# A two-layer decoder trunk: factors through the logarithm of k, transposes by transfers, guarded single buffers, and a new table of distances

## The chip, the cores and the metric

The kernel runs on one core of a Trainium2 chip. A core has a matrix engine (TensorE, "PE" in the profile, with its weight loads as "PEld"), three engines for elementwise work (VectorE "DVE", ScalarE "ACT", GpSimd "POOL"), and SyncE ("SP"), which here only issues transfers. Each engine works through a queue of its own in order, and they wait for one another by semaphores. Transfers are issued from SP's and ScalarE's queues ("SPq", "ACTq"). The metric is the device time of one execution in microseconds; lower is better.

## What is computed

Two layers over 256 tokens of width 2048, in float32. Each layer normalises the residual h, makes one wide input projection, feeds two groups of heads from it, and projects their outputs back:

```python
hn = rms_norm(h, norm_w[l])
proj = hn @ w_in[l]
y_a = deltanet_branch(...)          # 8 heads of 128, gated delta rule
y_b = hgrn2_branch(...)             # 8 heads of 128, gated linear recurrence
h = h + concatenate([y_a, y_b]) @ w_out[l]
gate = sigmoid(h @ w_ple_gate[l])
h = h + (p[l] @ w_ple_up[l]) * gate
...
return rms_norm(h, final_norm_w)
```

In the delta-rule branch ("DN") q and k are divided by their norms, so the sum of squares of each row of q is needed. In the HGRN2 branch ("HG") k = (1 - lb) sigmoid(-f), log f = log(lb + (1 - lb) sigmoid(f)), G is the running sum of log f, and the products inside a chunk are

```python
A = einsum("bhrd,bhsd,bhrsd->bhrs", q_c, k_c, exp(G_r - G_s))   # r >= s
```

## The kernel before

**Products.** The big projections are done in three products each: a weight tile is split into a high part `whi` (ScalarE, line 443) and a rest `wlo` (VectorE, line 445), the activations likewise, and TensorE sums high by high, high by low and low by high (line 381 is the helper that issues every product; line 384 is the helper that issues every transpose). The work is cut into *steps* of one weight tile: `run_step` issues the products of one step, mostly twelve of 128x512. `ahead` loads weight tiles through SP's queue four steps ahead (line 424) and splits them two steps ahead.

**Everything else is woven between the steps.** The mixers are Python generators that emit instructions and then yield a number of steps to wait, or a condition. `tick`, called after each step, counts them down and resumes those that are due. The numbers come from the tables `DELAY` (by kind of generator and place) and `DELAY_AT` (the same for one group, so `"h2u64"` is the place u64 of HG group 2). TensorE's instructions keep exactly the order in which they are emitted; the other engines' queues are ordered by the compiler's scheduler, by readiness and then by order of emission. Where the next step needs a tile that is not emitted yet, `while not pairs_ready(...): tick()` lets turns go by without a step.

**Transposes.** Activations must stand with channels on partitions. This is done in two ways: on TensorE against the identity (`turn`, `turned`, `stat`, and the end of `head_norm`), or by transfers. For the latter, `apart` (line 568) copies the float32 tile into two planes of 16-bit halves on ScalarE and writes them to memory from ScalarE's queue (line 569), and `across` (line 576) reads them back with a transposing transfer on SP's queue. The tuples `FQ_DMA`, `VC_DMA`, `PV_DMA` and `Y_DMA` name the groups that go by transfers. For the residual (`after_out`, which makes `g0` and `g1` for the gate, and `after_gate`, which makes `n1` for the next layer) the quarters c = 0, 1, 2 go by transfers and c = 3 on TensorE.

**DN.** Four groups of two heads in each layer. `decay` makes the table `Dt` (one buffer, tag "Dt"): two products by GpSimd, `pD` on TensorE, an exponential. `dkdq` applies the convolution and SiLU; `k_side` transposes k on TensorE (`ssk`) and scales it by `Dt`; `q_side` makes the Gram products `pg`, the matrix `Bt` and `QK` with `Dt`, then transposes q on TensorE (`ssq`), squares the rows on ScalarE (line 922) and makes `nq`, which scales the output. It then calls `inv.given`; when all four groups have given, `Inverse` runs: small products `pp16` to `px64` with copies between them (lines 776 to 850). After it each group runs its recurrence `pz0`, `pS`, `pw`, `pz1`, `po` and its norm.

**HG.** `f_side` makes k (tag "hk", one buffer) and G ("hG", one buffer); `q_side` makes, for each distance u = 2, 4, ..., 128, a tile of factors `X` (tag "hX", four buffers): two subtractions (lines 1159, 1161; for u = 128 a subtraction and a copy, line 1163), an exponential (line 1164), a multiplication of the lower half by k (line 1166) and of the upper half by q (line 1172). The products go to three banks, `pa` (u = 1 to 8), `pb` (16 to 64) and `pa128`.

Of the kernel before, what the change touches and what calls it, by code (L numbers as in the profile page):

```python
# [17 lines left out]
NG = 4  # L18
# [15 lines left out]
def chunk_cols(chunk):  # L34
# [5 lines left out]
DELAY = {  # L40
# [6 lines left out]
DELAY_AT = {  # L47
# [14 lines left out]
}  # L62


FQ_DMA = 0, 1, 2
VC_DMA = 0, 1
# [112 lines left out]
def trunk(ctx: ExitStack, tc: tile.TileContext, head, xT, x, pT, W, par, fw, cst, msk, eye, out):  # L179
# [137 lines left out]
    lnhd = cp.tile([128, 1], F32, name="lnhd")  # L317
    G.memset(lnhd, float(-0.5 * np.log(128.0)))
    mhalf = cp.tile([128, 1], F32, name="mhalf")
    G.memset(mhalf, -0.5)  # L320
# [96 lines left out]
    LOOK, LOAD = 2, 4  # L417
    state = dict(small=0, next=0, loaded=0, prepped=0, squared=0)

# [433 lines left out]
    class DN:  # L853
# [17 lines left out]
        def decay(self):  # L871

            g, n = self.g, self.n
            self.beta = self.row.beta[:, 4 * g:4 * g + 4]
            ugs = []
            for j in range(2):
# [38 lines left out]
        def stat(self, w, name, tiles=range(4)):  # L915

            ps = pm.tile([128, 512], F32, tag="m", name=self.n + name)
            for i in tiles:
                PE.transpose(ps[:, 128 * i:128 * i + 128], self.kq[i % 2][:, i // 2, w, :], ident)
            ss = small(name)  # L920
            for i in tiles:
                S.activation(sp.tile([128, 128], F32, tag="junk", name="junk", bufs=1), ps[:, 128 * i:128 * i + 128],
                             AF.Square, accum_out=ss[:, i:i + 1])
            return ps, ss

# [29 lines left out]
        def q_side(self):  # L955
            n, kq = self.n, self.kq
            yield self.wait("q")
# [24 lines left out]
            for hh, pg in enumerate(pgs):  # L982
                for t in range(2):
                    i = 2 * hh + t
                    V.scalar_tensor_tensor(Bt[:, i], pg[:, 256 * t:256 * t + 128], nb[:, i:i + 1], Dt[:, i],
                                           ALU.mult, ALU.mult)
                V.tensor_tensor(self.QK[:, 2 * hh:2 * hh + 2], pg.rearrange("p (t w c) -> p t w c", t=2, w=2)[:, :, 1, :],
                                Dt[:, 2 * hh:2 * hh + 2], ALU.mult)
            G.affine_select(self.QK, self.QK, pattern=[[0, 4], [1, 128]], compare_op=ALU.is_ge, fill=0.0, base=0,
                            channel_multiplier=-1)  # L990
            yield self.wait("ssq")
            pq, ss = self.stat(1, "ssq")
            lq = small("lq")
# [85 lines left out]
    class HG:  # L1079
# [9 lines left out]
        def wait(self, step):  # L1089
            return delay("h", self.g, step)  # L1090

        def hi(self, ps, c0):
            self.v = mix("iv", 512, 2, self.n + "iv")
            for t in range(2):
                S.activation(self.v[:, 256 * t:256 * t + 256], ps[t][:, c0:c0 + 256], AF.Copy, scale=self.row.rt[:, t:t + 1])
            self.done.add("i")
            yield 1

        def hfhq(self, ps, c0):
            et, _ = evict(ps, c0, 512, self.row.rt, self.n + "fq")  # L1100
            if self.g in FQ_DMA:
                x = yield from apart(et, self.n + "fq")
                yield self.wait("e")
                t = across(x, self.n + "fq")
                yield self.wait("c")
                spawn(self.f_side(t[:, 0:512]))
                spawn(self.q_side(t[:, 512:1024]))
            else:
                yield self.wait("p")
                spawn(self.f_side(turned(et, 0, self.n + "pf")))  # L1110
                spawn(self.q_side(turned(et, 256, self.n + "pq")))

        def f_side(self, fs):
# [10 lines left out]
            for m in range(2):  # L1124
                sl = slice(256 * m, 256 * m + 256)
                V.tensor_tensor_scan(self.G[:, sl], keep, sg[:, sl], 0.0, ALU.mult, ALU.add)
            self.done.add("f")
            yield self.wait("f")

        def q_side(self, qr):  # L1130
# [8 lines left out]
            yield self.after("f")  # L1139
            k, Gc = self.k, self.G  # L1140
            k4 = v4(k)
# [10 lines left out]
            def factors(us):  # L1152


                X = mix("hX", 512, 4, n + f"X{us[0]}")
                xs = [X[:, 512 * j:512 * j + 512] for j in range(len(us))]
                for u, x in zip(us, xs):
                    ends = lo(Gc, u)[:, :, u - 1:u].to_broadcast([128, 256 // u, u])
                    V.tensor_tensor(lo(x, u), ends, lo(Gc, u), ALU.subtract)
                    if u < 128:  # L1160
# [4 lines left out]
                for u, x in zip(us, xs):  # L1165
                    V.tensor_tensor(lo(x, u), lo(x, u), lo(k, u), ALU.mult)
                    hx = hi(x, u)
# [82 lines left out]
            for b in range(0, 128, 32):  # L1250
                S.copy(A[b:b + 32, :, b:b + 32], Ad[b:b + 32])
            xs = factors((128,))
            yield self.wait("u64")

# [63 lines left out]
    def after_out(c, ps, hact, l):  # L1318
        for m in range(2):
            V.tensor_tensor(h[c][:, m], ps[m], h[c][:, m], ALU.add)  # L1320
        if c < 3:
            hact[2 * c:2 * c + 2] = yield from turn_by_dma(c, f"g{l}", lambda kp: None)
# [4 lines left out]
    def after_gate(c, ps, up, act, st, l):  # L1327
# [21 lines left out]
        if l + 1 < DEPTH:  # L1349
            scales = lambda kp: norm_scales(l + 1, kp)  # L1350
            if c < 3:
                act[2 * c:2 * c + 2] = yield from turn_by_dma(c, f"n{l + 1}", scales)
# [227 lines left out]
```

## Time and profile before

| what | value |
|---|---|
| runs | 1213.8, 1214.54, 1216.82 us; median 1214.54 |
| the profiled execution | 1215.15 us, of which the span from the first to the last instruction is 1213.2 |
| granted TensorE clock, mean | 0.997 |
| moved by transfers | 252.24 MB, mean 208 GB/s |
| transfers of SP's and ScalarE's queues | 61.4% and 5.4% of 16 transfer engines' span |
| VectorE's and ScalarE's largest groups | the weight splits, 481.2 and 408.6 us |

Times in the profile are microseconds, "ns" where marked. Rows of groups read: line, engine, operation, output<-inputs, shapes, count, then busy time, mean of one, and idle time ahead of it with what ended it. Rows of waits read: who <- whom: total, times, longest. Rows of the timeline and of the chain begin with the start and the length. Rows of a tile give the shortest, middle and longest duration in ns, then first and last start. A name such as `hg12X` is HG, layer 1, group 2, tile X. Lengths of products are modelled by the profiler and overlap; distances between starts, and the chain, tell what a product holds TensorE for.

### The profile page before, as it was taken

To read this page: it belongs to the slowest core of one execution; us is meant where nothing else is said; L and a number is where in the kernel's file an instruction comes from. 1 tells how busy PE (TensorE), PEld (TensorE's weight loads), DVE (VectorE), ACT (ScalarE), POOL (GpSimd) and SP (SyncE) were. 2 spreads that over 40 slices of the span, in tenths; PEclk is the share of its full clock that TensorE was granted. 3 is DMA by queue.
4 is the path that set the end of the run, shared out by engine and by line. 5 is a ranking of instruction groups with operands and counts; after the bars stand their busy time and mean duration, and the time that the engine had idled before them with its cause. 6 is when DMAs were issued, how large, how long until landed. Compare 5 with 4: busy or idle time off the path is not lost. (4 is left out here: it accounts for less than half of the span.)

```text
span 1213.2 us, 21302 instructions
## 1 busy us (share of the span) xinstructions
PE 1198.1 (99%) x8098; PEld 997.9 (82%) x8098; DVE 877.1 (72%) x1537; ACT 825.3 (68%) x1424; POOL 78.1 (6%) x67
## 2 busy tenths in 40 slices
PE   9999999999899999999999999999999999999997
PEld 8888888888788888888788888888788888888886
DVE  8669796878768756546665888877897786665565
ACT  7578777678678755538656778766886776564553
POOL 1410000000000000000003100100000000000011
PEclk9999999999999999999999999999999999999999
DMA  8677756686655648756867777667756566596563
GB/s 313 200 244 226 239 191 212 210 239 175 204 174 174 192 157 257 237 191 191 260 213 221 228 231 232 190 192 222 213 171 188 155 193 209 173 279 212 180 205 122
DMA packets 150646, 252.24 MB, mean 208 GB/s; under 512 B 83472, under 2 KB 90000, under 8 KB 150544
## 3 DMA queue, kind: packets, MB, share of 16 engines
q1 hardware_dynamic: 130528, 228.71, 61.4%
q10 hardware_dynamic: 20016, 22.17, 5.4%
q8 instruction: 63, 1.03, 0.3%
q14 instruction: 39, 0.32, 0.1%
HBM read 212.84 MB, written 21.23 MB: 193 GB/s over the span
## 5 line engine op out<-in xcount | busy, mean ns | idle before, releaser
L445 DVE TENSOR_TENSOR wlo<-raw,whi 128x1024 fp32r<-128x1024 f32 (+2 forms) x393 | 481.2, 1229 | 255.8 <-ACT whi L443 247.6
L443 ACT ACTIVATE whi<-raw 128x1024 fp32r<-128x1024 f32 (+2 forms) x393 | 408.6, 1044 | 235.8 <-PE out L381 64.3
L381 PE MATMUL in1hf<-whi,n1hi 128*128 128x512 f32 x128 | 41.0, 402 | 0.8 <-ACT dn12zs L673 0.8
L381 PE MATMUL in1hi<-whi,n1hi 128*128 128x512 f32 x128 | 41.4, 404 | 0.0
L381 PE MATMUL gate<-whi,g0hi 128*128 128x512 f32 x128 | 39.7, 392 | 1.1 <-ACT pg L1334 1.1
L381 PE MATMUL in1dk<-whi,n1hi 128*128 128x512 f32 x128 | 39.9, 393 | 0.0
L381 PE MATMUL in1hi<-whi,n1lo 128*128 128x512 f32 x128 | 39.7, 391 | 0.0
L381 PE MATMUL in1hf<-whi,n1lo 128*128 128x512 f32 x128 | 39.6, 390 | 0.0
L381 PE MATMUL in1dk<-whi,n1lo 128*128 128x512 f32 x128 | 39.5, 390 | 0.0
L381 PE MATMUL gate<-whi,g0lo 128*128 128x512 f32 x128 | 39.4, 389 | 0.0
L381 PE MATMUL in1dv<-whi,n1hi 128*128 128x512 f32 (+1 forms) x128 | 36.6, 378 | 0.0
L381 PE MATMUL in1hf<-wlo,n1hi 128*128 128x512 f32 x128 | 35.7, 390 | 0.2 <-DVE wlo L445 0.2
L381 PE MATMUL gate<-whi,g1hi 128*128 128x512 f32 (+1 forms) x120 | 35.7, 379 | 0.0
L381 PE MATMUL gate<-wlo,g0hi 128*128 128x512 f32 x128 | 35.6, 390 | 0.1
L381 PE MATMUL gate<-whi,g1lo 128*128 128x512 f32 (+1 forms) x120 | 35.7, 379 | 0.0
L381 PE MATMUL in1hi<-wlo,n1hi 128*128 128x512 f32 x128 | 35.6, 390 | 0.0
L381 PE MATMUL in1dk<-wlo,n1hi 128*128 128x512 f32 x128 | 35.6, 389 | 0.0
L381 PE MATMUL in1dv<-whi,n1lo 128*128 128x512 f32 (+1 forms) x128 | 35.0, 365 | 0.0
L381 PE MATMUL gate<-wlo,g1hi 128*128 128x512 f32 (+1 forms) x120 | 32.4, 378 | 0.0
L381 PE MATMUL in1dv<-wlo,n1hi 128*128 128x512 f32 (+1 forms) x128 | 31.5, 363 | 0.0
L381 PE MATMUL in0hi<-whi,n0hi 128*128 128x512 f32 x96 | 30.9, 403 | 0.0
L381 PE MATMUL in0hf<-whi,n0hi 128*128 128x512 f32 x96 | 30.5, 399 | 0.0
(1404 smaller groups left out, 2890.0 us busy)
## 6 DMA issues: line engine op xcount, KB each, us to landing
raw<-W SPq DMA_DIRECT2D x383, 512.0 KB, 3.9
raw<-W SPq DMA_DIRECT2D x7, 544.0 KB, 5.3
h<-x SPq DMA_DIRECT2D x4, 512.0 KB, 4.9
xt<-xT SPq DMA_DIRECT2D x3, 512.0 KB, 5.6
out_dram<-h SPq DMA_DIRECT2D x5, 256.0 KB, 2.3
di0d<-di0Bt ACTq DMA_DIRECT2D x4, 256.0 KB, 2.3
di1d<-di1Bt ACTq DMA_DIRECT2D x4, 256.0 KB, 2.7
fw<-fw ACTq DMA_DIRECT2D x2, 512.0 KB, 3.9
```

Of the source, the lines that this page charges most:

```text
L381: return tc.keep_in_program_order(nc.tensor.matmul(*a, **k))
L443: S.activation(hi[:, sl], raw[:, sl], AF.Copy)
L445: V.tensor_tensor(lo[:, sl], raw[:, sl], hi[:, sl].bitcast(F32), ALU.subtract)
```

## The change

It has five parts.

1. HGRN2's factors hold k through its logarithm: `f_side` adds ln(k + 2^-120) and subtracts it from G into a new tile `Gk`; the lower halves then use `Gk` in place of G, and the multiplication by k at line 1166 goes. `hX` has three buffers in place of four.
2. q's row sums: in all four DN groups (`SSQ_DMA`) q's planes are copied apart by two strided copies, written, transposed by a transfer and squared from there, in place of `stat(1, "ssq")`.
3. The residual's last quarter: `G_DMA` and `N_DMA` name all four quarters, so `turn` is no longer used.
4. Single buffers guarded: `decay` waits until the group before has emitted its last use of `Dt` (`state["dn"]`), and HG's `f_side` and `q_side` start only when the group before has emitted its last factors (`state["hg"]`).
5. The tables of distances are filled anew.

```diff
-    "b2e": 6, "b2g": 6, "b2o": 2,
-    "b3g": 5, "b3o": 2, "b3t": 6,
...
+    "b0e": 9, "b0g": 5, "b0o": 2, "b0t": 5,
+    "b1e": 7, "b1g": 6, "b1o": 5, "b1t": 6,
+    "b2e": 15, "b2g": 6, "b2o": 2, "b2t": 5,
+    "b3e": 8, "b3g": 5, "b3o": 6, "b3t": 8,
...
+SSQ_DMA = 0, 1, 2, 3
+G_DMA = 0, 1, 2, 3
+N_DMA = 0, 1, 2, 3
...
             self.beta = self.row.beta[:, 4 * g:4 * g + 4]
+            yield lambda: state["dn"] == NG * self.l + g
...
+            state["dn"] += 1
             G.affine_select(self.QK, self.QK, pattern=[[0, 4], [1, 128]], compare_op=ALU.is_ge, fill=0.0, base=0,
                             channel_multiplier=-1)
-            yield self.wait("ssq")
-            pq, ss = self.stat(1, "ssq")
+            if g in SSQ_DMA:
+                rows = dr.tile([256 * 512], U16, tag="tr512", name=n + "qd", bufs=4)
+                flat = u16(tmp(n + "qpl"))
+                for t in range(2):
+                    S.copy(flat.rearrange("p (w h t c) -> p w h t c", w=2, h=2, t=2)[:, :, :, t],
+                           u16(kq[t]).rearrange("p h v (c w) -> p w h v c", w=2)[:, :, :, 1])
+                nc.scalar.dma_start(out=rows.rearrange("(p x) -> p x", p=128), in_=flat)
+                yield self.wait("qe")
+                pq = across((rows, 512, 512), n + "q")
+                yield self.wait("qt")
+                ss = self.sums(pq, "ssq", range(4))
...
+                yield self.turn_is_ours
                 spawn(self.f_side(t[:, 0:512]))
...
+            S.activation(sg, self.k, AF.Ln, bias=tiny)
+            self.Gk = mix("hGk", 512, 1, n + "Gk")
+            V.tensor_tensor(self.Gk, self.G, sg, ALU.subtract)
...
-                X = mix("hX", 512, 4, n + f"X{us[0]}")
+                X = mix("hX", 512, 3, n + f"X{us[0]}")
...
-                    V.tensor_tensor(lo(x, u), ends, lo(Gc, u), ALU.subtract)
+                    V.tensor_tensor(lo(x, u), ends, lo(Gk, u), ALU.subtract)
...
-                    V.tensor_tensor(lo(x, u), lo(x, u), lo(k, u), ALU.mult)
...
             xs = factors((128,))
+            state["hg"] += 1
...
-        if c < 3:
+        if c in G_DMA:
             hact[2 * c:2 * c + 2] = yield from turn_by_dma(c, f"g{l}", lambda kp: None)
...
-            if c < 3:
+            if c in N_DMA:
                 act[2 * c:2 * c + 2] = yield from turn_by_dma(c, f"n{l + 1}", scales)
```

More of the change, by code (lines that the diff above doesn't have):

```diff
@@ L318, in trunk @@
     G.memset(lnhd, float(-0.5 * np.log(128.0)))
+    tiny = cp.tile([128, 1], F32, name="tiny")
+    G.memset(tiny, float(2.0 ** -120))
     mhalf = cp.tile([128, 1], F32, name="mhalf")
@@ L417, in trunk @@
     LOOK, LOAD = 2, 4
-    state = dict(small=0, next=0, loaded=0, prepped=0, squared=0)
+    state = dict(small=0, hg=0, dn=0, next=0, loaded=0, prepped=0, squared=0)
     def load(n):
@@ L919, in stat, with sums @@
                 PE.transpose(ps[:, 128 * i:128 * i + 128], self.kq[i % 2][:, i // 2, w, :], ident)
+            return ps, self.sums(ps, name, tiles)
+        def sums(self, ps, name, tiles):
             ss = small(name)
@@ L923, in stat @@
                              AF.Square, accum_out=ss[:, i:i + 1])
-            return ps, ss
+            return ss
         def dkdq(self, ps, c0):
@@ L955, in q_side @@
         def q_side(self):
-            n, kq = self.n, self.kq
+            n, kq, g = self.n, self.kq, self.g
             yield self.wait("q")
@@ L988, in q_side @@
                                 Dt[:, 2 * hh:2 * hh + 2], ALU.mult)
+            state["dn"] += 1
             G.affine_select(self.QK, self.QK, pattern=[[0, 4], [1, 128]], compare_op=ALU.is_ge, fill=0.0, base=0,
                             channel_multiplier=-1)
-            yield self.wait("ssq")
-            pq, ss = self.stat(1, "ssq")
+            if g in SSQ_DMA:
[9 more added lines that the diff above has]
+                ss = self.sums(pq, "ssq", range(4))
+            else:
+                yield self.wait("ssq")
+                pq, ss = self.stat(1, "ssq")
             lq = small("lq")
@@ L1090, in wait, with turn_is_ours @@
             return delay("h", self.g, step)
+        def turn_is_ours(self):
+            return state["hg"] == NG * self.l + self.g
         def hi(self, ps, c0):
@@ L1109, in hfhq @@
                 yield self.wait("p")
+                yield self.turn_is_ours
                 spawn(self.f_side(turned(et, 0, self.n + "pf")))
@@ L1139, in q_side @@
             yield self.after("f")
-            k, Gc = self.k, self.G
+            k, Gc, Gk = self.k, self.G, self.Gk
             k4 = v4(k)
```

24 rows, old and new, of tables (DELAY, DELAY_AT) are left out of this document.

## The prediction

> **What bounds the kernel now.** I read the page first (engine totals, then the slices), then TensorE's waits, then pieces of the chain of work that ended last.
>
> ```profile
> span 1213.2 us, 21302 instructions
> ```
>
> Of this span the engines were busy:
>
> ```profile
> PE 1198.1 (99%) x8098; PEld 997.9 (82%) x8098; DVE 877.1 (72%) x1537; ACT 825.3 (68%) x1424; POOL 78.1 (6%) x67
> ```
>
> TensorE is busy 99% of the span; no other engine passes 72%. A busy share alone proves little, so the next view asks what TensorE ever waited for. These are all its waits of the whole execution:
>
> ```profile
> PE di0px L381 <- ACT di0P L840: 3.1, 2, 2.8
> PE gate L381 <- ACT pg L1334: 1.1, 1, 1.1
> PE warm L381 <- DVE zeros L256: 1.1, 1, 1.1
> PE in1hf L381 <- ACT dn12zs L673: 0.8, 1, 0.8
> PE hg03yp L384 <- DVE hg03yt L655: 0.3, 1, 0.3
> PE hg13yp L384 <- DVE hg13yt L655: 0.3, 1, 0.3
> PE in1hf L381 <- DVE wlo L445: 0.2, 1, 0.2
> PE in0dz L381 <- ACT n0ahi L281: 0.2, 1, 0.2
> ```
>
> They sum to 7.1 us. So the time is the sum of what stands in TensorE's queue, in the order the program writes out. Work taken off that queue is worth its full length; work taken off VectorE, ScalarE or the transfers is worth nothing unless one of these waits shrinks. The price of a piece comes from the chain, where lengths are TensorE time and not an instruction's own duration:
>
> ```profile
> 957.48 0.44 PE dn12pv L384 x4
> 957.92 2.77 PE in1dv L381 x12
> ...
> 1048.62 57.15 PE out L381 x252
> ...
> 1111.21 0.88 PE g1t L384 x8
> ```
>
> L384 is a transpose. Four take 0.44 us, eight take 0.88. Twelve weight products, one step of the loop, take 57.15 / 21 = 2.72 us undisturbed and 2.77 behind an insertion.
>
> **The change, part by part.** *q's row sums.* Eight groups (four pairs of heads, two layers) lose the transposes of `stat(1, "ssq")`:
>
> ```profile
> L384 PE MATMUL dn00ssq<-cs,dn00kq x4: 271/272/273, 109.0 to 109.3; 128*128 128x128 f32 x4
> ```
>
> Four starts within 0.3 us (0.1 apart), and the chain's 0.44 / 4 is 0.11 us each. 8 x 0.44 = 3.5 us leave TensorE. *The residual's last quarter.* `turn` for c = 3 goes in three places (g0, n1, g1) of eight transposes: 3 x 0.88 = 2.65 us. Together 56 transposes, 6.2 us; 11 fewer insertions at 0 to 0.05 us (2.77 against 2.72), taken as 0.03, add 0.3. No part adds a TensorE instruction. Sum so far: **-6.5 us**.
>
> The Trainium skill, page "TensorE: Matmul & The Clock Gate", Part 4, gives about 275 ns for a transpose inside a kernel. The durations above agree (272 ns), and by that price 56 would be worth 15.4 us; but starts 0.11 us apart show that they overlap, so the trace speaks against counting them so.
>
> *What replaces them.* Every transposed tile now goes through ScalarE copies into 16-bit planes, a write to memory, and a transposing transfer on SP's queue. The kernel already does this for three quarters:
>
> ```profile
> L568 ACT COPY n12pl<-h x2: 1030/1036/1042, 592.8 to 593.8; 128x1024 uint16<-128x1024 uint16 x2
> n11d<-n11pl ACTq DMA_DIRECT2D x2, 256.0 KB, 6.6
> g11tr<-g11d SPq DMA_TRANSPOSE x1, 8.2
> ```
>
> Residual: 6 copies x 1.04 = 6.2 us of ScalarE. Row sums: 16 strided copies of 512 values, not in the trace; between half the row above and all of it, 8 to 17 us. With the new logarithm of k below, ScalarE gets 20 to 28 us over the span, and the transfers carry some 7 MB more (8 x 0.25 and 3 x 0.5, written and read). What must hide it is slack beside TensorE, worst where the k/q chunks run:
>
> ```profile
> 60.00:160.00 100.00, 100.00 (x449) 82.81 (x449) 80.62 (x148) 78.94 (x139) 6.34 (x4) 1.00 0.75 237
> ```
>
> (columns: TensorE, weight loads, VectorE, ScalarE, GpSimd, clock, transfer share, GB/s.) ScalarE at 79% rises to about 86%, transfers at 0.75 by some 0.03. I take 0.
>
> Does the data come in time? A step being 2.72 us, I counted the steps between each hand-over in the code. q's row sums feed only `nq`, needed dozens of steps later at the DN output; but `given` now follows them, so the inverse starts three steps later (after step 66 of the run, was 63) and is ready after 105, was 100. The chain of the last DN group does not move: its first product stays after step 129, held by its own v, and its output transpose comes after step 138, was 139. So the later inverse is absorbed. The tightest transposed tile is the residual's last quarter ahead of layer 1:
>
> ```profile
> 614.58 0.69 DVE L1345 TENSOR_TENSOR h<-h,pg 128x512 f32<-128x512 f32 x1
> 602.76 1.71 ACT L533 ACTIVATE n1hi<-n12tr,pr 128x256 fp32r<-128x256 f32 x4 [2.02 <-DMA n12tr<-n12d]
> 634.88 0.66 PE L381 MATMUL in1dz<-whi,n1hi 128*128 128x272 f32 x4
> ```
>
> h is ready at 615.3; a copy behind other work (1 + 1.04), a write (6.6), a transpose (8.2, the longest of the residual's) and the split (1.71 on ScalarE and an estimated half us of VectorE behind it, from 0.69 for twice the columns) end at 634.3 at the worst; the product needs it at 634.0, as 0.88 us go. Cost 0 to 0.3 us; 0 taken. In the gate the same tile has 12 steps, 33 us: free.
>
> *HGRN2.* `lo(k)` no longer multiplies each factor:
>
> ```profile
> L1166 DVE TENSOR_TENSOR hg01X<-hg01X,hg01k x7: 417/420/422, 223.6 to 265.0; 128x256 f32<-128x256 f32 x7
> 314.23 0.63 ACT L1164 ACTIVATE hg02X<-hg02X 128x512 f32<-128x512 f32 x1 [3.08 <-DVE hg02X L1161]
> 314.88 1.18 ACT L840 COPY di0P<-di0pp 64x512 f32<-64x512 f32 x2
> ```
>
> VectorE loses 56 x 0.42 = 23.5 us and gains eight subtractions of 512 columns, at the price of the addition at 614.58 above, 8 x 0.69 = 5.5; ScalarE gains eight logarithms, at the price of the exponential of the same size, 8 x 0.63 = 5.0. All of it lies beside TensorE: worth 0, except that a VectorE chain ahead of a product gets shorter. But `hX` goes from four buffers to three. X16, X32 and X64 fill them, so X128 can start only when the bank `pb` has been multiplied. Before it ran ahead:
>
> ```profile
> 924.80 0.53 PE L381 MATMUL hg12pa<-hg12X 128*32 128x64 f32 x29
> 928.56 0.61 PE L381 MATMUL hg12pa<-hg12X 128*128 128x128 f32 x4
> L1172 DVE TENSOR_TENSOR hg12X<-hg12X,hg12q x7: 416/418/421, 889.8 to 921.7; 128x256 f32<-128x256 f32 x7
> ```
>
> X128's last multiplication started at 921.7, before `pb` ended at 925.3. Now subtraction, copy, exponential and multiplication (0.42 + 0.42 at most + 0.63 + 0.42 = 1.9 us bare, 5.0 with the longest hold above, 3.08) have to fit in the 3.2 us to 928.56. Only the third group has one step there; the others have two. Twice 0 to 1.8 us: 0 to 3.6; I take 0.8, nearer to the bare chain, since the program hands it to the queues ahead of its due time.
>
> *The guards* are waits of the program that emits the instructions, not of an engine; nothing queues behind them. A decay is now written only after the group before has used `Dt`, so D's product moves from after step 21 to after 44 and lands in one gap with the transposes of k and the Gram products: four of the five banks. Bounds 0 to 2 us (a bank freed one copy later); 0 taken, for the next request comes four steps later.
>
> *Distances anew.* Three effects on TensorE's order. The HG output in group 3 gets two steps to its transpose where one was: the two 0.3 us waits go, **-0.5**. The inverse's last hand-over to DN group 0 shrinks from two steps to one:
>
> ```profile
> 316.12 1.09 PE L381 MATMUL di0px<-di0Tt,di0P 64*32 64x64 f32 x62 [0.31 <-ACT di0P L840]
> 319.75 1.17 ACT L850 COPY di0Tt<-di0px 64x512 f32<-64x512 f32 x2
> 911.76 1.10 PE L381 MATMUL di1px<-di1Tt,di1P 64*32 64x64 f32 x64
> 916.54 1.18 ACT L850 COPY di1Tt<-di1px 64x512 f32<-64x512 f32 x2
> ```
>
> The copies end 3.7 and 4.9 us behind the product; with one step and a transpose (3.2 us) in between, TensorE would wait 0.5 and 1.7: 0 to 2.2, as ScalarE's order falls. I take 1.2. The 2.8 us wait for `di0P` has the same one step as before; in layer 1 that cost nothing. Gone or kept, -2.8 to 0; I take -1.4. Some distances overshoot what is left (c = 2 of the residual needs 23 turns where 16 steps remain, its `e` being 15), so `while not pairs_ready` makes 31 turns without products; by my count only splits, output transposes and one DN pair fall into them, none on a tight chain.
>
> Sum: -6.5 - 0.5 - 1.4 + 0.8 + 1.2 = **-6.4 us**. The profiled execution took 1215.15, so 1208.75; the median of the runs shown is 0.61 lower, 1214.54, so **1208.1 us**.
>
> **The rivals.** (1) *The gain is mostly given back*: the new tight places cost their upper bounds (3.6 + 2.2) and the old waits stay, -6.5 + 5.8 = -0.7, so 1213.8 from the median; for it, 31 idle turns and ScalarE at 86%; against, 7 us of waits in all of before. (2) *Weights late behind transposing transfers.* SP's queue issues both, and a transposing issue can stand in it:
>
> ```profile
> 467.97 2.73 SPq L576 DMA_TRANSPOSE g00tr<-g00d  x1
> 470.80 1.00 SPq L424 DMA_DIRECT2D raw<-W  x2
> 471.90 4.49 SPq L576 DMA_TRANSPOSE g01tr<-g01d  x1
> SPq L576 <- DMA n11d<-n11pl: 7.1, 1, 7.1
> 480.57 1.06 ACT L443 ACTIVATE whi<-raw 128x1024 fp32r<-128x1024 f32 x1 [0.46 <-DMA raw<-W]
> 1060.00:1110.00 50.00, 50.00 (x222) 41.39 (x222) 29.47 (x30) 25.84 (x28) 0.00 (x0) 1.00 0.86 258
> ```
>
> After two such issues from 468.0 to 476.4 a weight split was 0.46 us late and TensorE, two splits ahead (5.4 us), did not notice: a stop starts at about 8.4 - 0.46 + 5.4, or 13.4 us. g02 with g03 and n12 with n13 are now written back to back; a wait of 7.1 and two issues of 4.5 make 16.1, so 2.7 us in three places: 1208.1 + 8.1 = 1216.2. Against it stands the last row, a transfer share of 0.86 with TensorE busy all 50 us. The Trainium skill, "DMA: Bandwidth & Descriptors", section "Issuing engines are not separate DMA queues", says that all transfers share the same 16 engines whoever issues them, which speaks for this rival; no row here shows weights losing to a transpose by more than the 0.46 us.
>
> (3) *Slower: ScalarE's queue held by X128.* Its exponential waits for VectorE, which waits for `pb`; behind it stand the copies of `di0P` and `di0Tt`. Before, the hold of 3.08 us at 314.23 above, with the copy of `di0P` right behind it at 314.88, cost TensorE 2.8 us once. By the new order `pb` of group 2, the inverse's last two products, `pa128` and DN 0's first product lie within three steps. Held at all three hand-overs in both layers, 6 x 2.8 = 16.8, less the 3.1 there already: -6.5 + 13.7 = +7.2, so 1221.7 from the median. It decides from 3.2 us a layer. (4) *Each transpose is worth its duration*, 56 x 0.272 = 15.2, so 1199.3; the chain speaks against it.
>
> **How the numbers follow.** Forecast 1208.1 (1203 to 1211): 0.70. Rival 1: 0.16. Rival 2: 0.05. Rival 3: 0.07. Rival 4: 0.02. The range 1203 to 1216 takes in the forecast with all old waits gone (-6.5 - 4.5, so 1203.5) and rivals 1 and 2; about 0.1 and some tails lie outside. About 0.3% (3.6 us) is what a measurement of this kernel can tell from no change: faster (under 1210.9) 0.71, same 0.21, slower (over 1218.2) 0.08.
>
> **What would show it.** Transposes at L384's place: 88 where 144 stood, no `ssq`, `g0t`, `g1t`, `n1t` among TensorE's rows; TensorE's busy time down by 6 to 7 us and its list of waits between 4 and 9 us. VectorE down by about 18, ScalarE up by 20 to 28. Wrong would be waits of TensorE on `di0Tt`, `hg02X`, `hg12X`, `n13tr` or raw of over 3 us each, or a busy time that falls by another amount.

## The result and the profile after

The changed kernel takes **1204.27 us** (median of 5 runs, 1203.15 to 1208.85) where the kernel before took 1214.54: a ratio of 0.9919, 95% interval 0.9898 to 0.994, so 10.3 us faster. Forecast were 1208.1 us and a range of 1203 to 1216.

The page of the changed kernel, profiled in the slowest of these runs (1208.85 us), begins so:

```profile
span 1207.1 us, 21219 instructions
...
PE 1191.0 (99%) x8042; PEld 991.9 (82%) x8042; DVE 864.3 (72%) x1489; ACT 844.5 (70%) x1454; POOL 81.5 (7%) x68
```

TensorE is as full as before, with 56 instructions fewer: 88 transposes are left of 144. Its busy time fell by 7.1 us. VectorE fell by 12.8 and ScalarE rose by 19.2, without either showing in the time. The view of TensorE's waits (who, on whom, total, times, longest) now lists:

```profile
PE in1hi L386 <- DVE wlo L450: 1.8, 1, 1.8
PE gate L386 <- ACT whi L448: 1.5, 1, 1.5
PE in0hf L386 <- ACT hg00zs L678: 1.4, 1, 1.4
PE warm L386 <- DVE zeros L259: 1.1, 1, 1.1
PE in1hi L386 <- ACT dn11zs L678: 0.8, 1, 0.8
PE in1hi L386 <- ACT whi L448: 0.3, 1, 0.3
PE hg12pa L386 <- DVE hg12X L1201: 0.2, 1, 0.2
PE in0dz L386 <- ACT n0ahi L284: 0.2, 1, 0.2
```

(Line numbers are higher than before, by five in most helpers: L386 issues the products, L448 and L450 split the weights, L1201, before L1172, is the last multiplication of a factor tile.) The waits for `di0P` and for the HG outputs are gone. What is listed adds up to 7.3 us, about as much as before; in a repeated run nearer the median it is 4.7 (first experiment).

One thing can't be seen in a list of waits. The view by windows (start:end, length, busy time and instructions of TensorE, weight loads, VectorE, ScalarE, GpSimd, then the **granted clock**, transfer share, GB/s) shows for the kernel before, in two equal stretches, the first beginning 2.2 us behind the end, at 315.51, of the 2.8 us wait for `di0P`:

```profile
317.70:321.10 3.40, 3.40 (x9) 2.62 (x8) 2.50 (x4) 3.34 (x7) 0.00 (x0) 0.50 1.04 125
321.10:324.50 3.40, 3.40 (x17) 2.81 (x16) 1.63 (x2) 3.23 (x4) 0.00 (x0) 1.00 0.65 218
```

In the first, TensorE is "busy" all 3.40 us but counts 9 products instead of 17, at a granted clock of 0.50. About half the work in 3.4 us is 1.7 us lost, so the wait cost some 1.7 us more than its length. The mean clock of 0.997 hides this, and so does the list of waits. The profiled execution of the changed kernel has one such stretch too, behind the wait of 1.8 us for `wlo`:

```profile
876.40:879.80 3.40, 3.40 (x70) 2.84 (x62) 3.40 (x6) 3.40 (x6) 0.00 (x0) 0.50 0.75 223
879.80:883.20 3.40, 3.40 (x81) 2.79 (x80) 3.40 (x8) 3.13 (x6) 0.00 (x0) 1.00 0.76 189
```

### The profile page after: what moved, and what is told of

Same layout as the page of the kernel before. It is cut to its first block, busy times and chain, and to the rows that moved or that the text cites. A ratio compares the mean times of both kernels' runs of the same rounds, so it can differ in the third digit from the quotient of the medians.

```text
span 1207.1 us, 21219 instructions
## 1 busy us (share of the span) xinstructions
PE 1191.0 (99%) x8042; PEld 991.9 (82%) x8042; DVE 864.3 (72%) x1489; ACT 844.5 (70%) x1454; POOL 81.5 (7%) x68
## 3 DMA queue, kind: packets, MB, share of 16 engines
q8 instruction: 63, 1.03, 0.3%
## 4 chain that ended last, share of the span: by engine, by line
PE 88%; DVE 4%; DMA 4%; ACT 3%; issue 1%; SPq 0%; ACTq 0%; POOLq 0%; POOL 0%; DVEq 0%
PE out L386 14%; PE gate L386 11%; PE in0dk L386 7%; PE in1dk L386 7%; PE in0hf L386 7%; PE in1hf L386 7%; PE in0dv L386 6%; PE in1hi L386 6%; PE in0hi L386 6%; PE in1dv L386 4%; DMA raw<-W 2%; DVE wlo L450 2%; PE up L386 1%; PE in0dz L386 1%; PE in1dz L386 1%
## 5 line engine op out<-in xcount | busy, mean ns | idle before, releaser
L450 DVE TENSOR_TENSOR wlo<-raw,whi 128x1024 fp32r<-128x1024 f32 (+2 forms) x393 | 476.9, 1219 | 234.3 <-ACT whi L448 227.6
L448 ACT ACTIVATE whi<-raw 128x1024 fp32r<-128x1024 f32 (+2 forms) x393 | 407.9, 1043 | 215.0 <-PE out L386 50.1
L386 PE MATMUL in1hi<-whi,n1hi 128*128 128x512 f32 x128 | 42.5, 413 | 1.0 <-ACT dn11zs L678 0.8
L386 PE MATMUL gate<-whi,g0hi 128*128 128x512 f32 x128 | 39.6, 390 | 1.5 <-ACT whi L448 1.5
L386 PE MATMUL in1hf<-whi,n1hi 128*128 128x512 f32 x128 | 40.8, 400 | 0.1
L386 PE MATMUL in1hi<-whi,n1lo 128*128 128x512 f32 x128 | 40.1, 395 | 0.0
L386 PE MATMUL in1dk<-whi,n1hi 128*128 128x512 f32 x128 | 39.7, 391 | 0.0
L386 PE MATMUL in1hf<-whi,n1lo 128*128 128x512 f32 x128 | 39.6, 390 | 0.0
L386 PE MATMUL in1dk<-whi,n1lo 128*128 128x512 f32 x128 | 39.5, 390 | 0.0
L386 PE MATMUL gate<-whi,g0lo 128*128 128x512 f32 x128 | 39.4, 389 | 0.0
L386 PE MATMUL in1hi<-wlo,n1hi 128*128 128x512 f32 x128 | 35.7, 391 | 1.8 <-DVE wlo L450 1.8
L386 PE MATMUL in1dv<-whi,n1hi 128*128 128x512 f32 (+1 forms) x128 | 36.4, 376 | 0.0
L386 PE MATMUL gate<-wlo,g0hi 128*128 128x512 f32 x128 | 35.6, 390 | 0.1
L386 PE MATMUL gate<-whi,g1lo 128*128 128x512 f32 (+1 forms) x120 | 35.7, 378 | 0.0
L386 PE MATMUL gate<-whi,g1hi 128*128 128x512 f32 (+1 forms) x120 | 35.7, 378 | 0.0
L386 PE MATMUL in1hf<-wlo,n1hi 128*128 128x512 f32 x128 | 35.6, 389 | 0.0
L386 PE MATMUL in1dk<-wlo,n1hi 128*128 128x512 f32 x128 | 35.5, 389 | 0.0
L386 PE MATMUL in1dv<-whi,n1lo 128*128 128x512 f32 (+1 forms) x128 | 35.0, 365 | 0.0
L386 PE MATMUL gate<-wlo,g1hi 128*128 128x512 f32 (+1 forms) x120 | 32.4, 378 | 0.0
L386 PE MATMUL in1dv<-wlo,n1hi 128*128 128x512 f32 (+1 forms) x128 | 31.6, 364 | 0.0
L386 PE MATMUL in0hi<-whi,n0hi 128*128 128x512 f32 x96 | 31.0, 404 | 0.0
L386 PE MATMUL in0hf<-whi,n0hi 128*128 128x512 f32 x96 | 30.2, 396 | 0.0
```

What stands on the lines that cost most here:

```text
L386: return tc.keep_in_program_order(nc.tensor.matmul(*a, **k))
L448: S.activation(hi[:, sl], raw[:, sl], AF.Copy)
L450: V.tensor_tensor(lo[:, sl], raw[:, sl], hi[:, sl].bitcast(F32), ALU.subtract)
```

## The experiments

All were timed against the kernel before, whose median was 1214.6 to 1215.3 us each time. "Waits" is the sum of TensorE's list of waits, "half clock" the stretches at a granted clock of 0.50 ahead of the end of the span, both in the one profiled execution.

| run | what it is | median us | ratio to before, 95% | waits | half clock |
|---|---|---|---|---|---|
| before | | 1214.54 | | 7.1 | 1 |
| after | | 1204.27 | 0.9919 (0.9898 to 0.994) | 7.3 | 1 |
| e1_after_again | after, unchanged | 1204.28 | 0.9919 (0.99 to 0.9937) | 4.7 | 0 |
| e4_residual_back | after, residual's last quarter on TensorE | 1207.23 | 0.9934 (0.9918 to 0.995) | 3.6 | 0 |
| e3_residual_only | before, residual's last quarter by transfers | 1211.07 | 0.9969 (0.9958 to 0.9979) | 6.4 | 1 |
| e5_ssq_back | after, row sums on TensorE, early | 1226.34 | 1.007 (1.0041 to 1.0099) | 16.9 | 3 |
| e11_ssq_back_late | after, row sums on TensorE, at the old place in time | 1207.3 | 0.9949 (0.9931 to 0.9966) | 4.4 | 1 |
| e2_old_table | after with the old distances | 1221.12 | 1.0053 (1.0036 to 1.0069) | 15.0 | 2 |
| e14_log_only | before with the first part alone | 1241.7 | 1.0212 (1.0185 to 1.0239) | 29.7 | 5 |
| e6_k_multiplied | after, k multiplied in again | 1204.7 | 0.9904 (0.9881 to 0.9927) | 6.3 | 0 |
| e10_no_guards | after without guards | 1204.33 | 0.99 (0.9873 to 0.9926) | 4.8 | 1 |
| e7_p64_two | before, `di0P` with two steps | 1214.6 | 0.9997 (0.9981 to 1.0013) | 7.3 | 1 |
| e12_p64_z0 | before, `di0P` and `di0Tt` with two steps | 1213.2 | 0.9987 (0.9976 to 0.9998) | 6.4 | 0 |
| e13_v_later | after, v of DN group 0 two steps later | 1208.33 | 0.9943 (0.9922 to 0.9965) | 7.3 | 1 |

My theory after the result was that TensorE's queue sets the time (**Q**): the 56 transposes are worth about 6 us, and the rest is waits and the half clock behind them. Its main rival was that the new distances made the gain (**D**).

### The same kernel again

> The changed kernel, unaltered, profiled a second time. Theory Q (TensorE's queue): the 56 transposes are worth 6.5 us, and the rest of the 10.3 us between the medians is old waits of TensorE that no longer occur; the waits of 1.4 to 1.8 us that the first profile shows (wlo, whi, hg00zs) belong to that one execution, the slowest of five. So 1204 again, and in a profile of a usual execution TensorE's waits sum to 3 to 5 us instead of 8.0. Rival V: the waits are part of the schedule, come back in the same places, and the 10.3 us have another source; waits again 7 to 9 us at a time near 1204.

1204.28 us, the same median. (The 8.0 us in that text are 7.3 by the list above.) Three of its seven waits, 4.7 us in all, as theory Q had it:

```profile
PE in1hi L386 <- DVE wlo L450: 1.5, 1, 1.5
...
PE hg02pa L386 <- DVE hg02X L1201: 0.9, 1, 0.9
...
PE gate L386 <- ACT whi L448: 0.2, 1, 0.2
```

The wait for `wlo` comes back at the same place, at 872, but is 1.5 us here and no half clock follows. So single waits differ by up to 1.3 us from execution to execution of one program (the gate's 1.5 and 0.2), and only what repeats should be explained.

### The transposes, one part at a time

The residual's last quarter, taken back from the changed kernel and added alone to the kernel before:

```diff
-G_DMA = 0, 1, 2, 3
-N_DMA = 0, 1, 2, 3
+G_DMA = 0, 1, 2
+N_DMA = 0, 1, 2
```

> The changed kernel with the residual's last quarter back on TensorE. Theory Q: 2.7 us slower than the changed kernel, 1207, with 112 transposes. Rival W: within 0.5 us of the changed kernel.

> The kernel before with one edit: the residual's last quarter by transfers, old tables. Theory Q: 24 transposes and three insertions fewer, 2.65 + 0.1 = 2.7 us, so a ratio of 0.9977; busy time of TensorE 2.7 us lower. Rival W (transposes hidden anyway, or given back as waits for n13 or g03): within 0.5 us of before.

Back on TensorE it costs 2.95 us (1207.23 against 1204.28); alone on the kernel before it gains 3.5 us (interval 2.6 to 5.1). Forecast were 2.65 and three insertions, so the price of 0.11 us for a transpose agrees with both runs, and the transfers that take their place cost nothing that shows.

q's row sums, taken back:

```diff
-SSQ_DMA = 0, 1, 2, 3
+SSQ_DMA = ()
```

> The changed kernel with q's row sums taken back to TensorE (the 32 transposes of stat(1, ssq); the planes, writes and transposing transfers of q go). Theory Q (TensorE's queue: 8 x 0.44 us of transposes and 8 insertions at 0.03): +3.8 us, 1208.1; TensorE's list of waits within 1.5 us of the changed kernel's. Theory I (what matters is when the inverse starts: three steps earlier with the transposes, so its last products meet X128 and group 2's bank): over +6 us, with new waits on di0P, di1P, hg02X or hg12X of 2 us and more. Theory T (the transfers and copies that the change brought cost part of what it won): under +2.5 us.

This cost 22 us by the medians (18 by the ratios to before; its eight times scatter from 1218.9 to 1230.9), some six times the transposes. The longest waits:

```profile
PE hg02pa L386 <- DVE hg02X L1201: 5.6, 1, 5.6
PE di1px L386 <- ACT di1P L813: 3.8, 2, 2.9
PE in0hi L386 <- ACT whi L448: 3.1, 1, 3.1
```

VectorE's own timeline (start, length, instruction, idle time ahead and what ended it) shows how the first of them came about:

```profile
333.47 0.69 DVE L1049 TENSOR_TENSOR dn01R<-dn01pvtr,invn 128x512 f32<-128x512 f32 x1 [5.73 <-DMA dn01pvtr<-dn01pvd]
334.08 1.22 DVE L450 TENSOR_TENSOR wlo<-raw,whi 128x1024 fp32r<-128x1024 f32 x1
335.22 0.22 DVE L1218 COPY_PREDICATED hg02Ad<-ms,hg02pa 128x64 f32<-128x64 int32 x1
...
335.95 0.42 DVE L1189 TENSOR_TENSOR hg02X<-hg02G,hg02Gk 128x256 f32<-128x256 f32 x1
...
337.92 0.42 DVE L1201 TENSOR_TENSOR hg02X<-hg02X,hg02q 128x256 f32<-128x256 f32 x1 [1.34 <-ACT hg02X L1194]
```

The bank `pb` of this group had been multiplied by 329.9, so X128 could have begun. But VectorE works its queue in order, and ahead of X128 stood the multiplication for `dn01R`, which waited 5.73 us for a transposing transfer. Here the wait of TensorE names `hg02X`; most of it comes from a transfer, some places further back. Waits (16.9 against 4.7), stretches at half clock (two of 3.4 us and one of 6.8, so 6.8 us lost) and transposes (3.8 forecast) add up to 22.8; the two profiled executions (1226.82 and 1203.96) are 22.9 apart.

Is it the transposes, or that the inverse starts earlier without the way by transfers (its first operations on VectorE at 200, in the changed kernel at 215)? The next run keeps the transposes and gives them the steps that the way by transfers takes (the changed entries alone):

```diff
-SSQ_DMA = 0, 1, 2, 3
+SSQ_DMA = ()
-"d0ssq": 2   "d1ssq": 2   "d2ssq": 2    "d3ssq": 2
+"d0ssq": 5   "d1ssq": 8   "d2ssq": 11   "d3ssq": 8
```

> The changed kernel with q's row sums on TensorE again as in e5_ssq_back, but the number of steps ahead of them set to what the way by transfers takes (5, 8, 11 and 8 in groups 0 to 3, where 2 stood), so that the inverse starts when it does in the changed kernel. Theory I (the 22 us of e5_ssq_back are 3.8 us of transposes, and the rest is the inverse starting about 15 us earlier, at 200 where the changed kernel has 215, in the way of the factors): +3.8 us on the changed kernel, 1208.1, waits on hg02X under 1 us and no stretch at half clock that the changed kernel hasn't. Theory R (TensorE's transposes with ScalarE's squares right behind them are themselves what holds the factors): 1218 and more, the wait on hg02X over 3 us. Theory T (the copies and transfers that take their place cost part of the gain): 1205 to 1207.

1207.3 us: 3.0 more than the changed kernel. By this row of its waits

```profile
PE hg02pa L386 <- DVE hg02X L1201: 0.2, 1, 0.2
```

the 5.6 us on `hg02X` are 0.2. Theory I is borne out: 3 us of the 22 are transposes, 19 (15 by the ratios) are the place in time. Its interval of some 2 us to either side doesn't tell 3.0 from theory I's 3.8, nor from the upper end of theory T. Residual and row sums together are worth 6.0 us by the medians where 6.5 were forecast.

### The distances and the three buffers

All the new code with the old tables (`qe` and `qt` four steps each, their general value):

> The changed kernel with the old tables of distances (the new places qe and qt at their default 4). Theory Q: the transposes are gone all the same, so 6.5 us of the gain stay: 1208, plus whatever waits this order has, at most 1212; 88 transposes in TensorE's rows. Rival D (the gain is the new table's): 1213 to 1216.

1221.12 us. It is slower than the kernel before, which theory Q alone didn't allow, and slower than rival D had it. The same code is worth 16.8 us more with the new distances (1221.12 against 1204.28). The waits lie at the first products with X128 and at the evictions behind them:

```profile
PE hg11pa L386 <- DVE hg11X L1201: 2.4, 1, 2.4
PE in1hf L386 <- ACT hg11zs L678: 2.0, 1, 2.0
PE hg01pa L386 <- DVE hg01X L1201: 1.8, 1, 1.8
PE in0hf L386 <- ACT hg01zs L678: 1.5, 1, 1.5
```

Next the first part of the change by itself on the kernel before, which is ln(k), `Gk` and

```diff
-                X = mix("hX", 512, 4, n + f"X{us[0]}")
+                X = mix("hX", 512, 3, n + f"X{us[0]}")
```

> The kernel before with the first part of the change alone: factors through the logarithm of k, hX in three buffers; transposes, guards and distances as before. Theory Z (worth nothing beside TensorE): within 1 us of before, 1214. Theory X (X128 waits for the bank pb in group 2, as forecast): +0 to +3.6 us, waits on hg02X and hg12X only. Theory D (three buffers under the old distances also hold groups 0 and 1, as the waits of e2_old_table on hg11X, hg01X and hg00X did, 5.3 us together, and the evictions behind them): +6 to +10 us, with those three waits in the list.

26.6 us slower than its own median of before: more than the worst theory had. These are the longest waits:

```profile
PE hg02pa L383 <- DVE hg02X L1176: 7.2, 1, 7.2
PE hg11pa L383 <- DVE hg11X L1176: 5.3, 1, 5.3
PE hg10pa L383 <- DVE hg10X L1176: 4.0, 1, 4.0
PE hg00pa L383 <- DVE hg00X L1176: 3.6, 1, 3.6
PE gate L383 <- ACT whi L445: 2.6, 1, 2.6
```

With four buffers X128 ran ahead. In the kernel before, its subtraction, the last of the seven in this row, started at 315.9, well before `pb` ended at 328.5:

```profile
L1159 DVE TENSOR_TENSOR hg02X<-hg02G x7: 413/418/419, 283.9 to 315.9; 128x256 f32<-128x256 f32 x7
```

With three it has to wait until `pb` is done, and then it takes its turn behind whatever VectorE holds at that moment. In group 0 and in group 2 of this run that was:

```profile
213.65 1.46 DVE L745 TENSOR_TENSOR di0pr<-di0fx 128x121 f32<-128x121 f32 x1
...
215.95 0.43 DVE L1164 TENSOR_TENSOR hg00X<-hg00G,hg00Gk 128x256 f32<-128x256 f32 x1
...
219.67 0.42 DVE L1176 TENSOR_TENSOR hg00X<-hg00X,hg00q 128x256 f32<-128x256 f32 x1
```

```profile
337.85 0.69 DVE L1029 TENSOR_TENSOR dn01R<-dn01pvtr,invn 128x512 f32<-128x512 f32 x1 [4.64 <-DMA dn01pvtr<-dn01pvd]
...
340.33 0.42 DVE L1164 TENSOR_TENSOR hg02X<-hg02G,hg02Gk 128x256 f32<-128x256 f32 x1
```

In group 0 the inverse's first operations (`di0pr`) stand ahead of X128 and between its parts: `pb` ended at 210.9, the last multiplication at 220.1. In group 2, where `pb` ended at 332.3, it is `dn01R` again. With the new distances the inverse starts later (215 against 201 for the same code with the old ones), and TensorE's own products between the end of `pb` and `pa128` last 5.5 to 7.1 us in group 1 where they lasted 2.8, and 3.8 to 4.0 in group 2 where they lasted 3.2; groups 0 and 3 keep their 5.5 and 6.5. The repeated run of the changed kernel shows group 2:

```profile
321.58 0.43 DVE L1189 TENSOR_TENSOR hg02X<-hg02G,hg02Gk 128x256 f32<-128x256 f32 x1
...
323.54 0.42 DVE L1201 TENSOR_TENSOR hg02X<-hg02X,hg02q 128x256 f32<-128x256 f32 x1 [1.34 <-ACT hg02X L1194]
...
328.08 0.69 DVE L1049 TENSOR_TENSOR dn01R<-dn01pvtr,invn 128x512 f32<-128x512 f32 x1 [0.77 <-DMA dn01pvtr<-dn01pvd]
```

X128 is through before `dn01R` comes. Why e2_old_table, with the same three buffers and the old distances, is some 20 us faster than e14_log_only is clear for group 2 alone. There `pb` ended only at 340.1, when `dn01R` had gone:

```profile
332.46 0.69 DVE L1049 TENSOR_TENSOR dn01R<-dn01pvtr,invn 128x512 f32<-128x512 f32 x1 [2.06 <-DMA dn01pvtr<-dn01pvd]
```

That run has the guards and both ways by transfers besides, and which of them moves the groups apart stays open: they weren't tried one by one under the old distances. Nor were three buffers tried without the logarithm; that they are what holds X128 is read from these rows.

### The logarithm and the guards

```diff
-            S.activation(sg, self.k, AF.Ln, bias=tiny)
-            self.Gk = mix("hGk", 512, 1, n + "Gk")
-            V.tensor_tensor(self.Gk, self.G, sg, ALU.subtract)
...
+                    V.tensor_tensor(lo(x, u), lo(x, u), lo(k, u), ALU.mult)
```

> The changed kernel with k multiplied into each lower half again (56 multiplications of 0.42 us back on VectorE, the logarithm and the subtraction of f_side gone: VectorE +18 us, ScalarE -5 us); hX keeps three buffers. Theory B (all of it lies beside TensorE): within 1 us of the changed kernel, 1203.3 to 1205.3. Theory X (with three buffers the chain of X128 is bare ahead of pa128, and the multiplication lengthens it by 0.42 us, twice, and other factors of the first steps too): +1 to +3 us, waits of TensorE on hg02X and hg12X of 0.6 us and more each. Theory S (past 1.8 us such a wait is followed by a stretch at half clock): then +4 us and more.

1204.7 us, within theory B's range. Two of its waits,

```profile
PE hg02pa L386 <- ACT dn02zs L678: 1.3, 1, 1.3
...
PE hg12pa L386 <- DVE hg12X L1199: 0.9, 1, 0.9
```

are longer by 0.4 to 0.7 us than in the repeated run, as theory X had them; the median doesn't show it. With the new distances the logarithm is worth nothing that shows: 0.4 us by the medians, with an interval of nearly 3 us to either side. Four buffers together with the new distances weren't tried.

> The changed kernel without the two guards (a decay no longer waits for the group before to be through with Dt, HG's sides no longer wait for the factors of the group before). Theory G0 (guards are free, as forecast): within 1 us of the changed kernel, 1203.3 to 1205.3. Theory G1 (without them a tile is written while the group before still needs its buffer, so VectorE or ScalarE hold their queues for it and TensorE stops): +2 us and more, with waits of TensorE on dn..Dt, hg..k or hg..G tiles or on what stands behind them. Theory G2 (the guards themselves cost up to 2 us by crowding D's product with the Gram products): -1 to -2 us.

1204.33 us: guards cost nothing that shows, as forecast (the interval is some 3 us to either side). The profiled run still has `PE in1hi <- DVE wlo`, at 2.4 us, and a stretch at half clock behind it.

### What the wait for di0P was worth

One distance of the kernel before changed:

```diff
-    "i0p16": 1, "i0p64": 1, "i0t16": 4, "i0t64": 5,
+    "i0p16": 1, "i0p64": 2, "i0t16": 4, "i0t64": 5,
```

> The kernel before with one number changed: the inverse's hand-over in layer 0 from pp64's copies (di0P) to px64 gets two steps instead of one. Theory C (the wait for di0P cost its 2.8 us and, behind it, a stretch of about 3.4 us at half the granted clock, which the trace of before has at 317.7, so 1.7 us more): -4.5 us, 1210.1, no stretch at half clock near 317 and TensorE's listed waits 2.8 us shorter. Theory W (the wait was worth only its length): -2.8 us, 1211.8. Theory N (the wait moves to the next product of the chain, DN group 0's first, which comes one step later): 0 to -1 us, 1213.6 to 1214.6, with a new wait of over 1.5 us on di0Tt or on a later DN tile.

1214.6 us, no change, and theory N came true, by this row:

```profile
PE dn00pz L381 <- ACT di0Tt L850: 2.7, 1, 2.7
```

The wait moved one product down the chain, and the half clock with it (to 321.6). So the chain was too long by a whole step, not one place of it. With a second step there (`"d0z0": 2` added):

> The kernel before with two steps from di0P to px64, as in e7_p64_two, and besides two steps (one before) from the inverse's end to the first product of DN group 0, to which the wait had moved there (2.7 us, followed by a stretch at half clock). Theory C (the wait was worth its length and 1.7 us of half clock behind it): no wait on di0P or di0Tt of over 1 us, no stretch at half clock near 320, -4.5 us: 1210.1 against the median 1214.6 of before. Theory W (its length alone): -2.8 us, 1211.8. Theory N (the wait moves on once more, into the chain of the group's later products): within 1 us of before.

1213.2 us, 1.9 less than its own median of before (interval 0.2 to 2.9), which is none of the three theories as they stand. In the profiled execution (1210.6 us, the fastest of twelve) neither wait is left and the clock stays full:

```profile
317.70:321.10 3.40, 3.40 (x16) 2.47 (x15) 2.81 (x4) 3.38 (x6) 0.00 (x0) 1.00 0.69 190
```

But others came or grew, on evictions of other groups, and take back most of the length of the wait:

```profile
PE in1hf L381 <- ACT dn12zs L673: 1.8, 1, 1.8
...
PE in0hf L381 <- ACT dn02zs L673: 0.7, 1, 0.7
```

The list is 0.7 us shorter in all, and the 1.7 us of half clock are gone: 2.4 us, near the 1.9 measured. The granted clock of every execution says the same: its mean is 0.9980 over these twelve and 0.9964 over the nineteen of before beside them, which over the span (one less the clock, times the span) is 2.4 against 4.3 us, so 1.9 less. What was won is the half clock; the length of the one wait, 2.8, was not what it was worth.

### An attempt at the last wait

> The changed kernel with one distance more: in DN group 0 two steps more between the transposing transfer of v and its convolution. In the profiles of the changed kernel VectorE is busy without a break for some 14 us ahead of 872, the convolution of dn10v (six operations, 3.5 us by the group of line 912) among it, and TensorE then waits 1.5 to 1.8 us for wlo, the longest wait it has left; once of 1.78 us with a stretch at half clock behind it. R of that group is ready at 892.7 and needed at 920, so two steps (5.4 us) are free. Theory V (VectorE's row of work is what holds wlo): no wait on wlo over 0.5 us near 870, -1.5 us, 1202.8; -3.2 us against such runs as have the half clock. Theory M (another operation takes its place, or the convolution holds a later wlo or a factor): within 1 us of the changed kernel, with a wait elsewhere of 1 us and more. Theory W (the weights themselves come late there, by transfers): the wait stays.

The fourteen unbroken microseconds in that text are those of the run without guards; in the repeated run VectorE had two gaps there, of 0.66 and 1.15 us. The edit is `"d0vc": 5` for 3. It gave 1208.33 us, 4 us slower by the medians (2.9 by the ratios to before), more than any of the theories had. The wait for `wlo` did go, and another came, as theory M had it:

```profile
PE di1px L386 <- ACT di1P L813: 3.8, 1, 3.8
```

followed by a stretch at half clock at 902.2. ScalarE's copies of `di1P` began at 900.58, 1.4 us later than in the repeated run, while TensorE came to their product over 2 us earlier. What held them stands on VectorE:

```profile
894.07 0.69 DVE L1049 TENSOR_TENSOR dn10R<-dn10pvtr,invn 128x512 f32<-128x512 f32 x1 [4.07 <-DMA dn10pvtr<-dn10pvd]
```

In the repeated run this multiplication waited 2.14 us and started at 892.67. The later convolution made v's transfers later; `dn10R` itself had the time, as the text says, but the operations of group 2 behind it in VectorE's queue had not, nor had ScalarE, which stood 5.43 us (1.46 in the repeated run) for one of them. No version tried is faster than the changed kernel by more than its measurement tells.

## Why the prediction was right, and where it was not

- **What bounds.** TensorE's queue, right: it is 99% busy after, too. TensorE's busy time fell by 7.1 us, where 6 to 7 were forecast, between two executions with one stretch at half clock each, which counts as busy; in the repeated run, which has none, it fell by 9.3 (to 1188.8). What could be isolated of the work beside it shows no price of its own: the residual's transfers in e3_residual_only, VectorE's multiplications in e6_k_multiplied, within what their intervals can tell. The busy times came near: ScalarE +19.2 (20 to 28), VectorE -12.8 (-18). The 56 multiplications were priced at their length of 0.42, but the next operation on VectorE starts some 0.34 us after one and overlaps it, so by this estimate the busy time loses 19 and not 23.5.
- **Transposes**, -6.5 forecast: 2.95 and 3.0 by the medians, so -6.0 measured (by the ratios of the two runs to the changed kernel's, 1.8 and 3.6, so -5.4; each has an interval of some 2 us to either side).
- **HG's output**, -0.5: both waits are gone, 0.6 us, right.
- **The wait for `di0P`**, -1.4 as the middle of "gone or kept": this is the mis-sized term. The prediction could not tell gone from kept and took the middle. The wait went whole, 3.1 us by its row of before, and with it a stretch at half clock that the prediction had put at nothing, 1.7 us: -4.8. The granted clock of all executions bears out the second part: 0.9962 on average over 64 of the kernel before and 0.9975 over 11 of the changed kernel, 4.6 against 3.1 us lost. That the wait went was near, as the repeated run shows: the copies of `di0P` end at 327.26, their product starts at 327.42.

```profile
326.07 1.19 ACT L845 COPY di0P<-di0pp 64x512 f32<-64x512 f32 x2
327.42 1.10 PE L386 MATMUL di0px<-di0Tt,di0P 64*32 64x64 f32 x64
328.58 1.19 ACT L855 COPY di0Tt<-di0px 64x512 f32<-64x512 f32 x2
331.71 0.61 PE L386 MATMUL dn00pz<-dn00R,di0Tt 128*128 128x128 f32 x4
```

Which of the new distances took it away is not isolated: taking the wait away in the kernel before (e12_p64_z0) gave only 1.9 us, since other waits took most of its length back.

- **`di0Tt` to the first product of DN group 0**, +1.2: it costs 0. In the rows above the copies end at 329.77, 1.3 us behind the product (1.4 in layer 1), and the next product starts at 331.71. The 3.7 and 4.9 had been taken from before, where ScalarE had other work ahead of these copies.
- **X128 with three buffers**, +0.8: 0.2 in the profiled run of after and 1.1 in the repeated one. Right in size under the new distances, though the time that X128 has to fit in is 3.8 to 4.0 us and not the 3.2 of before, and its start waits behind weight splits, a mask and copies that the prediction left out: 0.87 us of the 1.1 are group 2 in layer 0, where X128 is through 4.8 us after `pb`.
- **Not foreseen:** `in1hi <- wlo`, 1.5 to 1.8 us, in each profiled run of the changed kernel. It lies where hg12's first factors, dn10v's convolution and the weight splits meet on VectorE.

The list for the repeated run: -6.0 - 0.6 (HG's output) - 4.8 + 1.1 + 1.5, and 1.2 less at the gate and at the `zs` evictions, are -10.0, against -10.3 between the medians (the two profiled executions, 1215.15 and 1203.96, are 11.2 apart). Of this list the transposes are isolated by experiments; the waits and the half clock are read from the traces, and the new distances weren't tried on the code of before. The forecast was 3.9 us short: the `di0P` term lacked 3.4 and the +1.2 didn't come, while the smaller terms nearly cancel.

"Distances anew" was forecast as "three effects on TensorE's order". That was too small a view of it, though the sum didn't suffer: the other parts need the new distances. Without them the same code costs 6.5 us instead of gaining 10.3 (e2_old_table), and the first part alone costs 26.6 (e14_log_only). The mechanism is that of **rival 3**, a queue held by X128, except that it is VectorE's as much as ScalarE's; its sign was right, and the new table is what kept it from happening.

**Rival 2** came in one place, and small. SP's queue stood 6.6 us for the planes of n11 to be written, the weights behind came late, and a weight split waited for them:

```profile
567.01 1.93 SPq L581 DMA_TRANSPOSE n11tr<-n11d  x1
575.11 1.06 ACT L448 ACTIVATE whi<-raw 128x1024 fp32r<-128x1024 f32 x1 [2.63 <-DMA raw<-W]
```

This is the wait of 1.5 us at the gate in the first profile after the change; in the repeated run it is 0.2. The change did not bring it: the kernel before has the same hold (7.1 us), a split 1.59 us late at 583.69, which the prediction overlooked, and the wait of 1.1 us at the gate. The 2.7 us in three places didn't come. **Rival 1** falls since the new tight places cost 1.1 us at most where it had 5.8 and the old waits went, **rival 4** with the measured price of the transposes.

## What to carry to other kernels

Where one engine is busy 99% of the time, price what leaves its queue by the distance between starts (0.11 us a transpose here, in keeping with three runs), and count the half clock behind a long wait as part of that wait. A buffer that lets work run ahead is slack in every in-order queue that the work passes: taking it away costs what stands ahead at that moment, a transfer too (7.2 us in one place), unless the distances are fitted to it at the same time. Moving one step of a chain moved the wait to another place in both runs that tried it (e7_p64_two, e13_v_later), so look first along the whole chain, and at what stands behind it in each queue.

## What the hardware showed that was not expected

**A wait of TensorE of about 2 us is followed by a stretch at half clock.** In the 14 profiles, leaving out the start and the end of the span, all 15 waits of 1.98 us and more have a stretch at a granted clock of 0.50 that begins at, or up to 2.2 us behind, the end of the wait (in four of the longest, inside it); of the 9 waits between 1.50 and 1.84 us 2 have one; of the 13 between 1.0 and 1.45 none. It lasts 3.41 us, in three cases 6.83. Of 17 products in 3.4 us at full clock, 9 are left (the rows at 317.70 and 321.10).

Length isn't all that decides. In every trace the changes of the granted clock lie whole multiples of 3.413 us apart (in e5_ssq_back stretches begin at 286.91, 338.11 and 897.90, which is 15 and 164 such periods apart), as if the clock were set once a period. Counted by the longest part of a wait inside one period of this grid, the 17 waits with a stretch have 1.77 us and more, but for one of 1.56 (the wait for `di0P` before), and the waits of 1.0 us and more without one have 1.50 and less, but for one of 1.76 (`wlo` in e4_residual_back). The longest wait without a stretch, 1.84 us on `hg01X` in e2_old_table, is cut by an edge of the grid into 0.81 and 1.03. So the same wait can cost 1.7 us more or not, by where it falls; this is read from the traces, and no run was made to test it.

The Trainium skill, "TensorE: Matmul & The Clock Gate", section "Why this matters for your kernels", advises against idle gaps of more than about 3 us between bursts, for one idle window takes the clock to half. The mechanism agrees with the traces here; the bound doesn't, since waits of 2.0 to 2.9 us had the same effect eight times and waits of 1.8 us twice.
